# Ten of eleven gate/up chunks as seven products, and down groups that accumulate on a residual copied into PSUM

## The chip, the core and the metric

The kernel runs on one core of a Trainium2 chip. The metric is the time of one execution on the device in microseconds (us); lower is better. The kernel before takes 2157.46 us, the median of three runs (2156.99 to 2157.65). The core has engines that each work through their own queue in order: TensorE (PE; PEld is its loading of weights), VectorE (DVE), ScalarE (ACT), GpSimd (POOL) and SyncE (SP, which here only issues DMAs). Matmuls accumulate in PSUM, which this kernel uses as eight banks of 128 partitions by 512 fp32 numbers.

## What is computed

One layer on x of 256 rows by 2048 columns, all in fp32:

```python
x = layer_norm(ALPHA * x + 0.5 * swiglu(x, ffn1_w1, ffn1_w3, ffn1_w2), ln1_g, ln1_b)
x = layer_norm(ALPHA * x + mixer(x, w_in, ..., w_out), ln2_g, ln2_b)
x = layer_norm(ALPHA * x + 0.5 * swiglu(x, ffn2_w1, ffn2_w3, ffn2_w2), ln3_g, ln3_b)
x = x + sigmoid(x @ w_ple_gate) * (p @ w_ple_proj)
# swiglu(x, w1, w3, w2) = (silu(x @ w1) * (x @ w3)) @ w2
```

w1 and w3 are 2048 x 5632 and w2 is 5632 x 2048. The mixer (a chunked mLSTM beside a stick-breaking attention, between large projections) lies between the two FFNs. The change is almost wholly inside the FFNs.

## The kernel before

**Numbers as pairs.** Each fp32 operand of a matmul is split in two parts, hi and lo, of the type fp32r. For a weight tile of 256 rows by 512 columns (held as 128 x 1024, 512 KB, loaded by one DMA), ACT writes hi (a cast, L1297) and DVE writes lo = raw - hi (L1301): together one *split*. For each 128-row half of the tile there are three matmuls, hi by hi, hi by lo and lo by hi (L1358 to L1360). The six matmuls of one tile against one block of activations are called a *unit* here. Activations are split the same way (L351 and L352, or L359 and L360 behind the four transposes of L357).

**Plain chunks.** The 5632 hidden columns are eleven chunks of 512. Computed plainly, the gate and up projections of a chunk are 16 weight tiles, and each is used by two units, one for each half of the 256 rows: 32 units, 16 splits.

**Sevens.** Gate and up of a chunk can instead be taken as one 2 by 2 block product in the Strassen-Winograd form: seven block products instead of eight, 28 units. Its weight operands are sums of tiles, each used by one unit only, so there are 28 splits, and the sums are made by DVE (L423, 128 x 1024 in SBUF) or by an accumulating DMA that GpSimd issues (L429). The activation side has sums too, made once for each 512 columns of x by four half-width DVE operations (L368, L369, L371, L372), called a *form turn* here. The products come out of PSUM through DVE additions (helper `both`, L633), and products 1 and 2 accumulate in one bank. Before, chunks 0 and 3 are plain and the other nine are sevens.

**Down.** The down projection of a chunk is 16 units with 8 splits, for the output in four column groups and two row blocks. Chunks go in pairs. When a group's bank is done, DVE adds half of it to the residual in SBUF (L685).

**Order.** Python code writes the instructions in the order in which each engine takes them. `main` is a list of units (up of chunk 0, gate of chunk 3, down of chunk 0, and so on); `side` is the nine sevens one behind the other. Behind gate of chunk 0 (16 units) the first 20 units of `main` (HEAD) go alone: the 16 of up of chunk 0 and four of gate of chunk 3. The rest is woven with `side` in proportion. A split is issued as soon as a place among the held splits is free (in an FFN up to 11 raw and 6 split tiles ahead, by the table HELD). Work with a delay (the `sched.spawn` calls, with times from the table DELAY) is put in when the sum of the units' nominal times has passed its due time. At the start of an FFN the activations themselves come in four column parts: in FFN1 they are loaded, in FFN2 they come from the layer norm, whose affine step on the residual is two DVE operations for each part and row block (L596, L598).

**The start.** PE runs 5 + 2 matmuls of ones (WARM, WARM2) before its first unit.

## Time and profile before

| | before |
|---|---|
| median of three runs | 2157.46 us (2156.99 to 2157.65) |
| the profiled execution, span from its first to its last instruction | 2156.9 us |
| the profiled execution's own time | its span; the median is 0.6 us above it |
| PE busy | 2147.3 us, 100% |
| DVE busy | 1897.9 us, 88% |
| ACT busy | 1342.0 us, 62% |
| POOL busy | 157.8 us, 7% |
| DMA | 538 MB, mean 249 GB/s |
| TensorE clock granted | 1.000 on average |

A row of the timeline is: start in us from the span's begin, duration, engine, line, operation, output<-inputs, sizes, number of equal instructions in the row, and in brackets the idle time before it with what ended it. A row of the costliest groups is: line, engine, operation, sizes and count, then busy us in all and the mean in ns of one, then idle time just before them and what ended most of it. A row of the windows is: the stretch, its length, and the busy us (with the count of instructions) of PE, PEld, DVE, ACT and POOL, the granted clock, the mean busy share of the 16 DMA engines and GB/s. Busy times of neighbours overlap a little (an instruction's end is counted to its last write), so the cost of one more instruction is read from the distance of starts in a row of equal ones.

### The profile page before, as it was taken

What the parts mean: (1) busy time and instruction counts of PE and PEld (TensorE: products, weight loads), DVE (VectorE), ACT (ScalarE), POOL (GpSimd) and SP (SyncE); (2) the same over time, 40 slices, a digit from 0 to 9 for tenths busy, and PEclk for the clock granted to TensorE, in tenths of its full rate; (3) what the DMA queues carried; (4) which work ended last, traced back from release to release, by engine and by line L of the source; (5) the groups of instructions that cost most, each with busy time, mean ns of one, the idle gap of its engine ahead of it and who ended that gap; (6) DMA issues with size and microseconds to landing.
All of it is one profiled execution on the core that took longest, in us unless ns stands there. A gap on an engine that the chain in (4) does not pass through costs nothing.

```text
span 2156.9 us, 27553 instructions
## 1 busy us (share of the span) xinstructions
PE 2147.3 (100%) x9758; PEld 1780.6 (83%) x9758; DVE 1897.9 (88%) x2093; ACT 1342.0 (62%) x1652; POOL 157.8 (7%) x186
## 2 busy tenths in 40 slices
PE   9999999999999999999999999999999999999999
PEld 7888888888888888888888888888888888888887
DVE  7899999999998898887888975799999999999974
ACT  6666666666665665677866563556656666656572
POOL 0011000011000000000000000001000011000000
PEclk9999999999999999999999999999999999999999
DMA  8899888999993667877888976579989999999652
GB/s 351 268 274 272 258 270 262 286 272 276 269 325 119 228 211 216 243 221 201 269 266 268 280 253 212 200 195 271 278 246 268 280 276 273 269 264 304 228 174 80
DMA packets 152250, 538.06 MB, mean 249 GB/s; under 512 B 17200, under 2 KB 21808, under 8 KB 152112
## 3 DMA queue, kind: packets, MB, share of 16 engines
q1 hardware_dynamic: 126480, 442.97, 58.5%
q0 software_dynamic: 25632, 93.33, 23.0%
q8 instruction: 76, 1.25, 0.2%
q14 instruction: 62, 0.51, 0.1%
HBM read 529.94 MB, written 6.29 MB: 249 GB/s over the span
## 4 chain that ended last, share of the span: by engine, by line
PE 96%; DVE 2%; issue 1%; ACT 0%; DMA 0%; SPq 0%; DVEq 0%; ACTq 0%
PE mm L1358 31%; PE mm L1360 31%; PE mm L1359 31%; PE ms L357 1%; DVE split L1301 1%; PE ms L566 0%; DVE temp L850 0%; DVE raw L423 0%; PE ms L1017 0%; PE ms L939 0%; PE ms L954 0%; PE ms L1047 0%; DMA big<-in_x_t_dram 0%; ACT split L1297 0%; DVE actT L352 0%
## 5 line engine op out<-in xcount | busy, mean ns | idle before, releaser
L1301 DVE TENSOR_TENSOR split<-raw,split 128x1024 fp32r<-128x1024 f32 (+1 forms) x1090 | 1277.7, 1210 | 130.4 <-ACT split L1297 121.3
L1297 ACT CAST split<-raw 128x1024 fp32r<-128x1024 f32 (+1 forms) x1090 | 1090.0, 1043 | 476.8 <-DVE raw L423 153.3
L1358 PE MATMUL mm<-split,actT 128*128 128x512 f32 x3064 | 1201.8, 392 | 2.8 <-ACT actT L351 1.9
L1360 PE MATMUL mm<-split,actT 128*128 128x512 f32 x3064 | 1188.9, 388 | 0.0
L1359 PE MATMUL mm<-split,actT 128*128 128x512 f32 x3064 | 1187.7, 388 | 0.4 <-DVE split L1301 0.3
L1360 PEld LDWEIGHTS mm<-split,actT 128*128 128x128 f32 x3064 | 576.1, 188 | 119.5 <-DVE actT L352 0.9
L1358 PEld LDWEIGHTS mm<-split,actT 128*128 128x128 f32 x3064 | 576.6, 188 | 117.5 <-ACT actT L351 2.2
L1359 PEld LDWEIGHTS mm<-split,actT 128*128 128x128 f32 x3064 | 576.9, 188 | 114.2 <-DVE split L1301 1.2
L423 DVE TENSOR_TENSOR raw<-raw 128x1024 f32<-128x1024 f32 x190 | 231.4, 1219 | 1.6
L429 POOL DMA_DIRECT2D raw<-in_ffn_w_dram x140 | 122.9, 1009 | 1243.1 <-DVE split L1301 1091.1
L359 ACT CAST actT<-ms 128x512 fp32r<-128x512 f32 x52 | 30.4, 586 | 96.0 <-PE ms L357 90.0
L685 DVE SCALAR_TENSOR_TENSOR big<-mm,big 128x512 f32<-128x512 f32 x112 | 76.4, 684 | 2.3 <-PE mm L1360 2.1
L633 DVE TENSOR_TENSOR temp<-mm,temp 128x512 f32<-128x512 f32 x108 | 73.1, 686 | 2.4 <-PE mm L1360 1.2
L429 POOL DMA_DIRECT2D raw<-in_w_in_dram x38 | 33.3, 1000 | 516.0 <-DVE split L1301 323.6
L292 ACT ACTIVATE temp<-mm 128x512 f32<-128x512 f32 (+1 forms) x36 | 20.3, 570 | 58.6 <-PE mm L1360 58.6
L360 DVE TENSOR_TENSOR actT<-ms,actT 128x512 fp32r<-128x512 f32 x52 | 35.6, 688 | 15.6 <-ACT actT L359 15.5
L352 DVE TENSOR_TENSOR actT<-temp,actT 128x512 fp32r<-128x512 f32 (+1 forms) x42 | 27.3, 675 | 17.3 <-ACT actT L351 17.2
L288 ACT ACT_TABLE_LOAD x30 | 38.5, 1283 | 0.5
L1162 DVE SCALAR_TENSOR_TENSOR big<-big,mm 128x512 f32<-128x512 f32 x8 | 5.5, 686 | 30.9 <-PE mm L1360 30.9
L351 ACT CAST actT<-temp 128x512 fp32r<-128x512 f32 (+1 forms) x42 | 24.7, 610 | 9.4 <-DVE temp L369 8.7
L1217 DVE TENSOR_TENSOR temp<-temp,big 128x512 f32<-128x512 f32 (+1 forms) x10 | 5.8, 583 | 26.4 <-ACT temp L292 26.4
L292 ACT ACTIVATE rstd<-mv,eps 128x1 f32<-128x1 f32 x6 | 1.8, 295 | 42.7 <-DVE mv L549 42.7
(127 smaller groups left out, 601.7 us busy)
## 6 DMA issues: line engine op xcount, KB each, us to landing
raw<-in_ffn_w_dram SPq DMA_DIRECT2D x528, 512.0 KB, 6.0
raw<-in_w_in_dram SPq DMA_DIRECT2D x168, 512.0 KB, 5.1
raw<-in_ffn_w_dram POOLq DMA_DIRECT2D x140, 512.0 KB, 9.5
raw<-in_w_in_dram POOLq DMA_DIRECT2D x38, 512.0 KB, 8.5
raw<-in_w_out_dram SPq DMA_DIRECT2D x32, 512.0 KB, 4.6
raw<-in_w_ple_gate_dram SPq DMA_DIRECT2D x32, 512.0 KB, 4.3
raw<-in_w_up_m_dram SPq DMA_DIRECT2D x16, 512.0 KB, 6.2
raw<-in_w_up_sb_dram SPq DMA_DIRECT2D x16, 512.0 KB, 4.5
```

The source lines that it names most:

```text
L288: nc.scalar.preload_act_table_set(table[0])
L359: nc.scalar.copy(dst[:, 0], ps[:])
L360: nc.vector.tensor_tensor(out=dst[:, 1], in0=ps[:], in1=dst[:, 0], op=ALU.subtract)
L423: nc.vector.tensor_tensor(out=out.tile[:, :, :cols], in0=a.tile[:, :, :cols], in1=b.tile[:, :, :cols], op=ALU.add)
L429: nc.gpsimd.dma_start(out=whole(out.tile[:]), in_=whole(src), accum_op=ALU.add)
L633: nc.vector.tensor_tensor(out=out, in0=a, in1=b, op=op)
L685: nc.vector.scalar_tensor_tensor(out=xs, in0=ps, scalar=0.5, in1=xs, op0=ALU.mult, op1=ALU.add)
L1297: nc.scalar.copy(hi[:, ks], r[:, ks])
L1301: nc.vector.tensor_tensor(out=lo[:, ks], in0=r[:, ks], in1=hi[:, ks], op=ALU.subtract)
L1358: nc.tensor.matmul(ps, hi, w[0][:, k, :u.cols], start=first, stop=False, skip_group_check=u.onto)
L1359: nc.tensor.matmul(ps, hi, w[1][:, k, :u.cols], start=False, stop=False, skip_group_check=u.onto)
L1360: nc.tensor.matmul(ps, lo, w[0][:, k, :u.cols], start=False, stop=last, skip_group_check=u.onto)
```

## The change

In both FFNs only chunk 0 stays plain, and chunk 3 becomes a seven as well. The order of the units is written anew: gate of chunk 0 (16 units), two units of its up projection, the other 14 woven with the first 24 units of the sevens, 8 units of sevens alone, down of chunk 0 woven with the next 34, then each down pair woven with 56 units of sevens. Product 4 accumulates in the bank of product 7, after DVE has added a sum to that bank in place (`both(held[7], held[7], r["u"], ALU.add)`); product 2 now comes before product 4. The down groups start from a bank into which ACT has copied the residual (`seed`, up to five units ahead, while fewer than seven banks are in use), and ACT copies the result back (`put`), so that DVE's L685 is gone; the residual is kept twice as large for this and the last pair's copy halves it. In each seven, but for chunk 1, one sum of tiles that an accumulating DMA made is made by DVE. The mixer's projections that use `seven` get the same treatment of product 4. WARM2 is 11 instead of 2.

```diff
-HEAD = 20
+HEAD = 2
+LAG = 10
+TURNED = 32
+SEED_AHEAD = 5
-WARM2 = 2
+WARM2 = 11
...
@@ load_rows: the residual as it is read
-        activate(res[t, k][:], res[t, k][:], ACT.Copy, scale=ALPHA)
+        activate(res[t, k][:], res[t, k][:], ACT.Copy, scale=2.0 * ALPHA)
@@ four transposes into one bank, only the first with start
+    def turn_four(ps, src):
+        for k in range(4):
+            nc.tensor.matmul(ps[:, k], src[:, k * P:(k + 1) * P], ident[:], is_transpose=True,
+                             start=k == 0, stop=k == 3, skip_group_check=True)
@@ group
+            for u in pairs[-1]:
+                u.onto = seed is not None
+                u.seed = seed if i == 0 else None
@@ seven
-        accs[2] = accs[1]
+        accs[2], accs[4] = accs[1], accs[7]
...
-            m2 = Weight(b21, [], [b21])
-            m4 = Weight(b11, [b21], [b11], plus(b11, b11, b21), m6)
+            m2 = Weight(b21, [b21], [])
+            m4 = Weight(b11, [], [b11, b21], plus(b11, b11, b21), m6)
+            m4.needs = [b21]
...
-            then += [unit(4, i, m4, act, 1, 2), unit(2, i, m2, act, 0, 2)]
-            then[-1].onto = True
+            then += [unit(2, i, m2, act, 0, 2), unit(4, i, m4, act, 1, 2)]
@@ up7: what is done with the products
                 elif m == 2:
                     r["g0"] = temp()
                     activate(r["g0"][:], ps, ACT.Silu)
-                    sched.spawn(late(r["u"], r["v"], r["z"], r["g0"]), DELAY["late" if c < n - 1 else "last"])
...
                 elif m == 4:
+                    activate(r["u"][:], ps, ACT.Silu)
+                    sched.spawn(late(r["u"], r["v"], r["z"], r["g0"]), DELAY["late" if c < n - 1 else "last"])
+                elif m == 3:
                     sched.until(lambda: "rest" in r)
-                    both(r["u"][:], ps, r["u"][:], ALU.add)
-                    sched.spawn(silu(r["u"]), DELAY["silu"])
-                elif m == 3:
                     both(r["v"][:], ps, r["v"][:], ALU.subtract)
 
             def rest():
-                both(r["u"][:], held[7], r["u"][:], ALU.add)
-                both(r["z"][:], held[5], r["u"][:], ALU.add)
+                both(r["z"][:], held[7], r["v"][:], ALU.add)
+                both(held[7], held[7], r["u"][:], ALU.add)
                 r["rest"] = True
...
-            return seven(..., (range(c == 1, 4), range(c == 1, 4)))
+            return seven(..., (range(c == 1, 4), range(1, 4)))
@@ down
-                def add(ps, t, g=g):
-                    xs = xres(t, g * COL)
-                    nc.vector.scalar_tensor_tensor(out=xs, in0=ps, scalar=0.5, in1=xs,
-                                                   op0=ALU.mult, op1=ALU.add)
+                def put(ps, t, g=g):
                     if n - 1 in chunks:
+                        activate(xres(t, g * COL), ps, ACT.Copy, scale=0.5)
                         norm.chunk(t, g)
+                    else:
+                        nc.scalar.copy(xres(t, g * COL), ps)
+
+                def seed(ps, t, g=g):
+                    nc.scalar.copy(ps, xres(t, g * COL))
@@ the order of an FFN
-        gate, hidden = zip(*(up(c) for c in (0, 3)))
-        program.extend((skewed(gate[0][:SKEW]) if skew else flat(gate[0][:SKEW])) + flat(gate[0][SKEW:]))
-        main = flat(hidden[0] + gate[1] + down(0) + hidden[1] + down(1, 2) + down(3, 4) + down(5, 6) + down(7, 8))
-        side = in_line([up7(c) for c in (1, 2, 4, 5, 6, 7, 8, 9, 10)])
-        program.extend(main[:HEAD] + weave(main[HEAD:], side))
+        gate, hidden = up(0)
+        program.extend((skewed(gate[:SKEW]) if skew else flat(gate[:SKEW])) + flat(gate[SKEW:]))
+        side = in_line([up7(c) for c in range(1, n)])
+        program.extend(flat(hidden)[:HEAD])
+        program.extend(weave(flat(hidden)[HEAD:], side[:24]) + side[24:TURNED])
+        main, side = flat(down(0)), side[TURNED:]
+        for c in range(1, n - 2, 2):
+            at = 56 + (LAG - TURNED) * (c == 1)
+            program.extend(weave(main, side[:at]))
+            main, side = flat(down(c, c + 1)), side[at:]
+        program.extend(weave(main, side))
@@ the driver's loop over units
+    def open_bank(u):
+        u.acc["ps"] = ps_pool.tile([P, COL], F32, name="mm", tag="ps")
+        live.add(id(u.acc))
+        if u.seed:
+            u.seed(u.acc["ps"][:, :u.cols], u.tt)
+
+    def seeds_due(n):
+        for u in units[n:n + SEED_AHEAD]:
+            if u.seed and "ps" not in u.acc and len(live) < PSUM_BUFS - 1:
+                open_bank(u)
...
-            first, last = u.start and k == 0, u.stop and k == 1
+            first, last = u.start and k == 0 and not u.seed, u.stop and k == 1
```

Over the whole program the instructions change as follows: PE has 48 matmuls of 128x512 fewer (9000 to 8952) and nine matmuls of ones more; DVE has 24 splits more (1070 to 1094), 34 sums of tiles more (190 to 224) and about 125 operations of 512 columns fewer (L685's 112 to 5 among them); ACT has 24 casts more, 112 copies from SBUF into PSUM more, and about 119 copies or activations from PSUM more; GpSimd issues 2 accumulating DMAs fewer.

Two places show how the order on DVE moves. The first is the start of FFN1, right behind the first form turn (the four rows with `temp<-big` or `temp<-temp,big` are such a turn); `split<-raw,split` are weights' lo parts, `raw<-raw` sums of weight tiles, `actT<-temp,actT` lo parts of forms. Before:

```order
L1301 TENSOR_TENSOR split<-raw,split 128x1024 x5
L352 TENSOR_TENSOR actT<-temp,actT 128x512 x2
L1301 TENSOR_TENSOR split<-raw,split 128x1024 x2
L368 TENSOR_TENSOR temp<-big 128x256
L369 SCALAR_TENSOR_TENSOR temp<-temp,big 128x256
L371 TENSOR_TENSOR temp<-big 128x256
L372 TENSOR_TENSOR temp<-big,temp 128x256
L1301 TENSOR_TENSOR split<-raw,split 128x1024 x2
L352 TENSOR_TENSOR actT<-temp,actT 128x512 x2
L1301 TENSOR_TENSOR split<-raw,split 128x1024 x2
```

After (L1317 is the former L1301, L438 the former L423, L358 the former L352, L378 to L382 the form turn):

```order
L1317 TENSOR_TENSOR split<-raw,split 128x1024 x2
L438 TENSOR_TENSOR raw<-raw 128x1024
L1317 TENSOR_TENSOR split<-raw,split 128x1024 x2
L438 TENSOR_TENSOR raw<-raw 128x1024 x2
L1317 TENSOR_TENSOR split<-raw,split 128x1024
L358 TENSOR_TENSOR actT<-temp,actT 128x512 x2
L1317 TENSOR_TENSOR split<-raw,split 128x1024 x2
L378 TENSOR_TENSOR temp<-big 128x256
L379 SCALAR_TENSOR_TENSOR temp<-temp,big 128x256
L381 TENSOR_TENSOR temp<-big 128x256
L382 TENSOR_TENSOR temp<-big,temp 128x256
L1317 TENSOR_TENSOR split<-raw,split 128x1024 x4
```

Between the first form turn and the second, DVE had seven splits and has seven splits and three sums of tiles now.

The second place is the start of FFN2, where the affine steps of the layer norm (`big<-big`) go on among the first weights. Before, up to the operation ahead of the first form turn there:

```order
L596 SCALAR_TENSOR_TENSOR big<-big 128x512
L598 SCALAR_TENSOR_TENSOR big<-big 128x512
L1301 TENSOR_TENSOR split<-raw,split 128x1024 x2
L596 SCALAR_TENSOR_TENSOR big<-big 128x512
L598 SCALAR_TENSOR_TENSOR big<-big 128x512
L1301 TENSOR_TENSOR split<-raw,split 128x1024 x2
L596 SCALAR_TENSOR_TENSOR big<-big 128x512
L598 SCALAR_TENSOR_TENSOR big<-big 128x512
```

After:

```order
L609 SCALAR_TENSOR_TENSOR big<-big 128x512
L611 SCALAR_TENSOR_TENSOR big<-big 128x512
L1317 TENSOR_TENSOR split<-raw,split 128x1024
L438 TENSOR_TENSOR raw<-raw 128x1024
L1317 TENSOR_TENSOR split<-raw,split 128x1024
L609 SCALAR_TENSOR_TENSOR big<-big 128x512
L611 SCALAR_TENSOR_TENSOR big<-big 128x512
L1317 TENSOR_TENSOR split<-raw,split 128x1024
L438 TENSOR_TENSOR raw<-raw 128x1024 x2
L1317 TENSOR_TENSOR split<-raw,split 128x1024
L609 SCALAR_TENSOR_TENSOR big<-big 128x512
L611 SCALAR_TENSOR_TENSOR big<-big 128x512
```

Three sums of tiles now stand among the affine steps and ahead of the first form turn of FFN2, where there was none; the splits in this piece are four in both.

50 lines of the change are left out of this document (26 added, 24 removed).

## The prediction

> **What bounds the kernel now.** I read the busy times first, then the chain of waits, then the costliest groups of instructions.
>
> ```profile
> PE 2147.3 (100%) x9758; PEld 1780.6 (83%) x9758; DVE 1897.9 (88%) x2093; ACT 1342.0 (62%) x1652; POOL 157.8 (7%) x186
> PE 96%; DVE 2%; issue 1%; ACT 0%; DMA 0%; SPq 0%; DVEq 0%; ACTq 0%
> L1301 DVE TENSOR_TENSOR split<-raw,split 128x1024 fp32r<-128x1024 f32 (+1 forms) x1090 | 1277.7, 1210 | 130.4 <-ACT split L1297 121.3
> L423 DVE TENSOR_TENSOR raw<-raw 128x1024 f32<-128x1024 f32 x190 | 231.4, 1219 | 1.6
> L685 DVE SCALAR_TENSOR_TENSOR big<-mm,big 128x512 f32<-128x512 f32 x112 | 76.4, 684 | 2.3 <-PE mm L1360 2.1
> ```
>
> PE sets the time: it is busy all of the span and 96% of the chain is its own. A busy PE need not be a fast one, so I look at its pitch in mid FFN1.
>
> ```profile
> 419.81 0.39 PE L1358 MATMUL mm<-split,actT 128*128 128x512 f32 x1
> ...
> 427.97 0.39 PE L1358 MATMUL mm<-split,actT 128*128 128x512 f32 x1
> ```
>
> Between these starts lie 36 matmuls: 8.16/36 = 0.2267 us each, so a unit of six takes 1.360 us. A matmul taken away is worth that, as long as DVE, second with 88%, can feed the rest. Windows of 10 us at the start of FFN2 show what that mean hides.
>
> ```profile
> 1390.00:1400.00 10.00, 10.00 (x45) 8.29 (x45) 9.86 (x13) 5.04 (x6) 0.00 (x0) 1.00 0.61 208
> 1400.00:1410.00 10.00, 10.00 (x45) 8.27 (x44) 9.97 (x16) 7.24 (x9) 0.00 (x0) 1.00 0.36 121
> 1410.00:1420.00 10.00, 10.00 (x46) 8.28 (x45) 9.93 (x17) 3.04 (x4) 1.75 (x2) 1.00 0.54 116
> 1420.00:1430.00 10.00, 10.00 (x50) 8.29 (x49) 10.00 (x12) 8.51 (x11) 0.00 (x0) 1.00 0.68 188
> ```
>
> Both are full (PE's 10.00, DVE's 9.86 to 10.00): DVE works 39.8 of 40 us and PE has not yet had to wait. More DVE work per unit of PE becomes time here, once the slack is used.
>
> **What one DVE instruction costs.** Busy times of neighbours overlap, so I take distances between starts.
>
> ```profile
> 32.91 4.63 DVE L1301 TENSOR_TENSOR split<-raw,split 128x1024 fp32r<-128x1024 f32 x4 [0.22 <-DMA raw<-in_ffn_w_dram]
> 37.46 1.29 DVE L352 TENSOR_TENSOR actT<-temp,actT 128x512 fp32r<-128x512 f32 x2
> 38.67 2.36 DVE L1301 TENSOR_TENSOR split<-raw,split 128x1024 fp32r<-128x1024 f32 x2
> ...
> 1397.97 0.69 DVE L596 SCALAR_TENSOR_TENSOR big<-big 128x512 f32<-128x512 f32 x1
> 1398.69 0.69 DVE L598 SCALAR_TENSOR_TENSOR big<-big 128x512 f32<-128x512 f32 x1
> 1399.30 0.42 DVE L368 TENSOR_TENSOR temp<-big 128x256 f32<-128x256 f32 x1
> ...
> 1400.77 2.35 DVE L1301 TENSOR_TENSOR split<-raw,split 128x1024 fp32r<-128x1024 f32 x2
> ```
>
> Four splits take 37.46 - 32.91 = 4.55, 1.137 each. A sum of tiles (L423) has the same size and mean (1219 against 1210 ns), so 1.137 too. A 512-column operation takes (38.67 - 37.46)/2 = 0.605 (0.607 over many pairs, which I use). An affine pair is 1399.30 - 1397.97 = 1.33, a form turn 1400.77 - 1399.30 = 1.47.
>
> **How far DVE is ahead of PE at these places.** The lead is the start of the matmul that needs a split less the end of that split; the smallest in a unit counts.
>
> ```profile
> 31.47 1.23 DVE L1301 TENSOR_TENSOR split<-raw,split 128x1024 fp32r<-128x1024 f32 x1 [5.43 <-ACT split L1297]
> 34.01 0.39 PE L1359 MATMUL mm<-split,actT 128*128 128x512 f32 x1
> ...
> 1381.04 0.69 DVE L352 TENSOR_TENSOR actT<-big,actT 128x512 fp32r<-128x512 f32 x1 [1.85 <-ACT actT L351]
> 1383.72 0.39 PE L1360 MATMUL mm<-split,actT 128*128 128x512 f32 x1
> ...
> 1426.54 2.35 DVE L1301 TENSOR_TENSOR split<-raw,split 128x1024 fp32r<-128x1024 f32 x2
> 1429.30 0.39 PE L1359 MATMUL mm<-split,actT 128*128 128x512 f32 x1
> ```
>
> In FFN1, at its 19th unit (the third of chunk 0's up projection, where the new order starts to differ), the lead is 34.01 - 32.70 = 1.3. In FFN2, ten units after its first, it is 1383.72 - 1381.73 = 2.0. It can't be larger in FFN1, since DVE stood idle for 5.43 just before, waiting for ACT. The third pair tests the tally: from 1381.73 to the end of the first split of the last DVE row (1427.76) the order has 19 splits and 3 sums (25.0), 12 operations of 512 columns (7.3), six affine pairs (8.0) and four form turns (5.9), 46.2 in all; the trace has 46.03.
>
> **PE's part.** 48 matmuls fewer: 48 x 0.2267 = -10.9. All 48 lie in the FFNs (four units each).
>
> **The start.** PE runs nine matmuls of ones more before its first unit.
>
> ```profile
> 1.13 3.35 PE L1235 MATMUL ms<-ones 128*128 128x128 f32 x14 [1.13 <-DVE ones L296]
> 6.35 0.80 PE L1358 MATMUL mm<-split,actT 128*128 128x512 f32 x1 [1.87 <-ACT actT L351]
> ...
> 12.07 0.53 PE L1359 MATMUL mm<-split,actT 128*128 128x512 f32 x1
> 12.43 0.40 PE L1360 MATMUL mm<-split,actT 128*128 128x512 f32 x1
> 12.67 0.40 PE L1358 MATMUL mm<-split,actT 128*128 128x512 f32 x1
> ```
>
> The seven of before are 14 records in 3.35, so nine are 18 records: 4.3 at that pace, against an idle gap of 1.87. From 6.35 to 12.43 there are 14.2 pitches of 0.427, then 0.23: a slow clock, ended by work. The bounds: 2.4 lost, if the added matmuls only push the first unit back (4.3 - 1.87), to 2.9 won, if all fourteen slow matmuls come at 0.227. I take -1.0. It reaches past the next term, since ACT's silu behind gate 0 waits for PE and DVE waits for ACT:
>
> ```profile
> 29.91 0.60 ACT L292 ACTIVATE temp<-mm 128x512 f32<-128x512 f32 x1 [6.36 <-PE mm L1360]
> ```
>
> **The start of FFN1.** Behind gate 0's 16 units there were 20 plain ones alone; now the sevens are woven in behind two. A seven's unit needs its own split, and sums beside it; a plain unit shares its split with another. I count DVE's instructions in the order from the one needed at the 19th unit to the one needed at the 91st (before the first product 4 of chunk 2, where the excess is largest): 62 splits and 17 sums (79 x 1.137 = 89.8), 25 operations of 512 columns (15.2) and three form turns (4.4): 109.4. PE's part is 72 units (97.9) and four groups of transposes.
>
> ```profile
> 405.28 0.60 PE L357 MATMUL ms<-ident,temp 128*128 128x128 f32 x4
> 405.63 0.47 PE L1358 MATMUL mm<-split,actT 128*128 128x512 f32 x1
> 405.95 0.39 PE L1359 MATMUL mm<-split,actT 128*128 128x512 f32 x1
> ```
>
> One group puts the second matmul behind it at 405.95 instead of 405.28 + 0.23, so 0.44; PE has 97.9 + 1.8 = 99.7. DVE needs 9.7 more than PE and has a lead of 1.3: PE waits **8.4**. Before, the same 72 units needed 52 splits, 11 sums, 22 operations and three turns, 89.4, which PE's 98.8 covered.
>
> **The start of FFN2.** The same order, with the layer norm's affine steps on top. From the 11th unit to the 91st DVE has 66 splits and 17 sums (94.4), 26 operations of 512 columns (15.8), six affine pairs (8.0) and four form turns (5.9): 124.1. PE has 80 units and the transposes, 108.8 + 1.8 = 110.6. The excess is 13.5, the lead 2.0: PE waits **11.5**. Most comes in one wait: the 23rd unit is the first that needs a form, and up to it DVE has 25.4 where PE has twelve units, 16.3, so the wait there is 25.4 - 16.3 - 2.0 = 7.1. Before, no form was needed in the first 36 units.
>
> **What moves and costs nothing.** Over the program DVE gains 24 splits and 34 sums (58 x 1.137 = 66) and loses about 125 operations of 512 columns, 107 of them L685 (76): lighter by 10, so behind the two starts it stays near its present share. The in-place sum in PSUM (`mm<-mm,temp`) is not in the trace: between 0.607 and a split's 1.137; I take 0.607 (same columns); there are two in each stretch, 1 more at most. ACT's 112 seeds are not in the trace either (a copy into PSUM): between 0 more and the 1.05 of a cast twice as wide.
>
> ```profile
> L1297 ACT CAST split<-raw 128x1024 fp32r<-128x1024 f32 (+1 forms) x1090 | 1090.0, 1043 | 476.8 <-DVE raw L423 153.3
> L639 ACT COPY temp<-mm 128x512 f32<-128x512 f32 x18 | 10.6, 586 | 15.7 <-PE mm L1360 15.6
> ```
>
> By the 586 ns of a copy from PSUM, 112 seeds and 119 put-backs are 135 and 24 casts 25: ACT goes from 1342 to about 1500, 70%. Behind a seed on ACT wait casts, and so splits; with 30% idle I cost it at nothing. Without that cover each seed and put-back would put the casts behind it off by 1.2, 130 over both FFNs.
>
> DMA: the FFN1 stretch issues two more loads on SP's queue and three more accumulating ones on POOL's than the same units before.
>
> ```profile
> 25.00:135.00 110.00, 110.00 (x491) 91.08 (x490) 98.11 (x106) 69.37 (x80) 10.59 (x12) 1.00 0.90 287
> ```
>
> Five transfers of 524 KB at 287 GB/s are 9 us beside 0.90 of 98.8; the stretch is longer by 8.4, so the share is about 0.91. It hides.
>
> **The sum.** 2157.46 - 10.9 - 1.0 + 8.4 + 11.5 = 2165.5. The profiled execution's span, 2156.9, lies 0.6 below the median; I carry that along.
>
> **The rivals.**
>
> *PE's count decides (faster or the same).* DVE's excess at the two starts would be absorbed, for instance by splits made further ahead while PE still works through gate 0 and the mixer's tail. For it: DVE is 88% busy over all, and 10 more of lead at each place would do. Against it: the window rows at FFN2's start, full already, and the 5.43 idle that DVE spends on ACT. Whole: 2157.46 - 11.9 = 2145.6; half absorbed: 2155.6.
>
> *PE waits for the bank of product 7 (slower still).* Product 4 may start only after DVE's in-place sum, which stands behind product 6's two sums and a difference: four operations (2.4) and a split or two (1.1 to 2.3), against about four units in between, product 3's last and product 2's first with those woven among them (5.4). Where it doesn't fit, 0.5 to 1 us in each of 20 sevens of the FFNs and five of the mixer: 12 to 25 on top, 2178 to 2190. It decides once DVE is more than 2 late there. For it, DVE's share in the FFNs:
>
> ```profile
> 100.00:200.00 100.00, 100.00 (x446) 82.85 (x446) 96.97 (x97) 64.26 (x70) 12.24 (x14) 1.00 0.93 278
> 400.00:500.00 100.00, 100.00 (x450) 82.86 (x450) 94.32 (x94) 61.86 (x66) 8.78 (x10) 1.00 0.91 272
> ```
>
> Against: 3.5 to 4.7 of work fit in 5.4.
>
> *The pause slows the clock.* The 7.1 wait in FFN2 could bring back the 0.427 pitch that followed the idle 1.87 at the start; by those rows, up to 14 matmuls at 0.2 more, 2.9: 2168.4. The Trainium skill ("TensorE: Matmul & The Clock Gate", section "What's actually happening") says that an idle window of about 3.4 us halves the clock and as long a busy one restores it; the rows at the start agree with a slow clock after idling, and no row of before shows a pause of that length later on.
>
> That the change doesn't do what it says is out: the order shows the 48 matmuls gone.
>
> **How the numbers follow.** Forecast 0.55 (2165.5; own range 2161 to 2171, from the start's -2.9 to +2.4, the in-place sum's 1 in each stretch and a lead 1 to 2 off), PE's count 0.24 (a third of it whole, two thirds part), the bank 0.13, the clock 0.08. The range reaches to half of the first rival and to the lower half of the bank's: 2149 to 2175. A measurement of this kernel can tell 0.2%, 4.3 us: faster is below 2153.1, slower above 2161.8. Faster: half of PE's count, 0.14. Same: the rest of it and the forecast's lower edge, 0.16. Slower: 0.70.
>
> **What would show it.** PE's matmuls 48 fewer at the same 0.227 pitch. PE idle, released by DVE splits or forms, between 35 and 135 and in the first 110 of FFN2, 8 and 11 in sum, one wait of some 7 at the first form of FFN2, and hardly any elsewhere; DVE at 9.9 of 10 there. No wait of PE on ACT's seeds. Wrong if PE is full in these windows (then DVE was ahead by more, or its work lies elsewhere in time), or if it waits at each product 4.

## The result

The changed kernel takes 2181.8 us (median of four runs, 2178.35 to 2184.69), the kernel before 2157.2 in the same runs: 1.0114 times as long, 95% interval 1.0102 to 1.0126. The forecast was 2165.5, slower, in a range of 2149 to 2175. The direction was right, the size was not: +24.6 instead of +8.

The runs of the change scatter over 6 us, those of before over 1. The profiled execution of the change is its fastest, 2178.35 (span 2176.3); the time outside the span is 2.0 us in it, as in other runs, and the profiled execution of before was itself some 1.7 us slower in its span than the runs that were timed.

The busy times and the chain of waits of the change:

```profile
PE 2148.7 (99%) x9728; PEld 1775.6 (82%) x9728; DVE 1891.6 (87%) x2026; ACT 1473.2 (68%) x1903; POOL 155.8 (7%) x184
PE 83%; DVE 7%; DMA 5%; issue 4%; ACT 1%; POOL 0%; SPq 0%; DVEq 0%; POOLq 0%; ACTq 0%
```

PE's share of the chain fell from 96% to 83%. What it waits for (engine and line, what ended the wait, then us in total, number, longest), of the change and then of before:

```profile
PE mm L1390 <- ACT actT L357: 8.2, 3, 4.8
PE ms L362 <- DVE actT L370: 6.4, 5, 2.2
PE mm L1392 <- DVE actT L358: 3.1, 3, 1.7
PE mm L1390 <- ACT mm L698: 1.8, 1, 1.8
```

```profile
PE mm L1358 <- ACT actT L351: 1.9, 1, 1.9
PE ms L1235 <- DVE ones L296: 1.1, 1, 1.1
PE mm L1358 <- DVE actT L1053: 0.9, 1, 0.9
```

Before, PE waited 4 us in all. Now it waits for forms (L357, L358), for banks that transposes need (L362 behind L370) and once for a seed (L698).

To see where time goes, I take for a stretch the distance between the starts of its first and last unit, less the work in it (0.2267 for each matmul of 512 columns, 0.11 for each transpose); what is left is called its loss here. For the change's two critical stretches:

```profile
32.30 0.39 PE L1390 MATMUL mm<-split,actT 128*128 128x512 f32 x1
...
146.15 0.39 PE L1390 MATMUL mm<-split,actT 128*128 128x512 f32 x1
...
1393.63 0.39 PE L1390 MATMUL mm<-split,actT 128*128 128x512 f32 x1
...
1517.53 0.50 PE L1390 MATMUL mm<-split,actT 128*128 128x512 f32 x1
```

146.15 - 32.30 - 99.7 = 14.2 in FFN1 (units 19 to 91) and 1517.53 - 1393.63 - 110.6 = 13.3 in FFN2 (units 11 to 91). The same for all stretches and profiles that the text speaks of:

| profile | FFN1 19-91 | FFN1 91-151 | rest of FFN1 | FFN2 11-91 | FFN2 91-157 | rest of FFN2 |
|---|---|---|---|---|---|---|
| before | 0.1 | 0.1 | 0.4 | 0.0 | 0.1 | 1.1 |
| the change | 14.2 | 2.4 | 1.4 | 13.3 | 1.9 | 0.6 |
| the change, second profile (e1) | 13.9 | 5.0 | 0.5 | 14.0 | 2.3 | 4.9 |
| e2: nine sevens | 0.1 | 0.1 | 1.8 | 0.0 | 0.2 | 1.9 |
| e7: nine, product 4 as before | 0.1 | 0.1 | 0.4 | 0.0 | 0.1 | 0.8 |
| e5: without eight sums an FFN | 12.8 | 4.7 | 1.5 | 12.0 | 1.9 | 2.4 |
| e9: without early accumulating loads | 10.4 | 0.3 | 0.9 | 13.1 | 0.3 | 1.0 |
| e17: their traffic without the wait | 10.4 | 0.3 | 1.7 | 13.0 | 1.7 | 1.1 |
| e10: without either | 4.8 | 0.1 | 1.5 | 9.1 | 0.1 | 1.1 |
| e3: affine steps later | 13.8 | 4.5 | 1.7 | 18.5 | 3.9 | 0.6 |
| e11: forms earlier | 11.8 | 4.0 | 0.4 | 17.6 | 2.3 | 0.9 |
| e12: both | 11.9 | 2.7 | 1.3 | 18.6 | 2.1 | 4.1 |
| e15: put back by DVE | 13.9 | 1.8 | 1.7 | 18.1 | 1.8 | 2.8 |

The mixer between the FFNs differs by less than 0.4 among these profiles. The account of the profiled execution closes: start -1.5, matmuls -10.9, the six columns' differences to before +14.1, +2.3, +1.0, +13.3, +1.8 and -0.5, together 19.6, against 2176.3 - 2156.9 = 19.4.

**FFN2's wait for the first form.** DVE, ACT and PE of the change:

```profile
1408.51 2.35 DVE L438 TENSOR_TENSOR raw<-raw 128x1024 f32<-128x1024 f32 x2
...
1414.77 2.35 DVE L1317 TENSOR_TENSOR split<-raw,split 128x1024 fp32r<-128x1024 f32 x2
1417.04 1.29 DVE L358 TENSOR_TENSOR actT<-temp,actT 128x512 fp32r<-128x512 f32 x2
```

```profile
1409.72 0.39 PE L1392 MATMUL mm<-split,actT 128*128 128x512 f32 x1
1414.89 0.79 PE L1390 MATMUL mm<-split,actT 128*128 128x512 f32 x1 [4.78 <-ACT actT L357]
1415.48 0.63 PE L1391 MATMUL mm<-split,actT 128*128 128x512 f32 x1
1417.78 0.79 PE L1392 MATMUL mm<-split,actT 128*128 128x512 f32 x1 [1.67 <-DVE actT L358]
```

PE loses 1414.89 - 1409.72 - 0.23 = 4.9 and 1417.78 - 1415.48 - 0.23 = 2.1: 7.0, where the forecast had 7.1, at the unit that it named. DVE runs without a gap there (from 1395 to 1495 it is busy for 99.45 of 100). Behind the wait the matmuls come at 0.43 for some 5 us, and the windows show the clock:

```profile
60.00:80.00 20.00, 16.89 (x65) 13.18 (x64) 18.23 (x22) 11.36 (x14) 0.90 (x2) 0.87 0.85 246
1400.00:1420.00 20.00, 13.55 (x52) 10.37 (x51) 19.83 (x25) 12.09 (x14) 1.75 (x2) 0.82 0.60 157
```

**FFN1 is another matter.** In the first of these two windows DVE is not full: 18.2 of 20. ACT and PE around the second form there:

```profile
68.51 1.05 ACT L1313 CAST split<-raw 128x1024 fp32r<-128x1024 f32 x1 [4.61 <-DMA raw<-in_ffn_w_dram]
71.54 1.99 ACT L1313 CAST split<-raw 128x1024 fp32r<-128x1024 f32 x2 [1.98 <-DMA raw<-in_ffn_w_dram]
73.44 1.14 ACT L357 CAST actT<-temp 128x512 fp32r<-128x512 f32 x2
```

The form turn was done on DVE at 68.5, but its cast on ACT (L357) stands in the queue behind the casts of weights, and these wait 4.61 and 1.98 for a loaded tile. DVE's half of the splits waits for the same casts. The chain of waits has a load of 11.8 us there, from 59.71 to 71.47: an accumulating one, issued by GpSimd at 59.16.

### The profile page after: what moved, and what is told of

Read it like the earlier page. It is cut to its first block, busy times and chain, and to the rows that moved or that the text cites. A ratio compares the mean times of both kernels' runs of the same rounds, so it can differ in the third digit from the quotient of the medians.

```text
span 2176.3 us, 27666 instructions
## 1 busy us (share of the span) xinstructions
PE 2148.7 (99%) x9728; PEld 1775.6 (82%) x9728; DVE 1891.6 (87%) x2026; ACT 1473.2 (68%) x1903; POOL 155.8 (7%) x184
## 4 chain that ended last, share of the span: by engine, by line
PE 83%; DVE 7%; DMA 5%; issue 4%; ACT 1%; POOL 0%; SPq 0%; DVEq 0%; POOLq 0%; ACTq 0%
PE mm L1390 27%; PE mm L1392 27%; PE mm L1391 26%; DMA raw<-in_ffn_w_dram 5%; DVE split L1317 4%; PE ms L362 1%; DVE raw L438 1%; ACT split L1313 1%; DVE actT L358 0%; DVE temp L866 0%; DMA big<-in_x_t_dram 0%; POOL raw L444 0%; DVE temp L646 0%; PE ms L1033 0%; PE ms L955 0%
## 5 line engine op out<-in xcount | busy, mean ns | idle before, releaser
L1317 DVE TENSOR_TENSOR split<-raw,split 128x1024 fp32r<-128x1024 f32 (+2 forms) x1114 | 1306.9, 1210 | 147.1 <-ACT split L1313 138.9
L1313 ACT CAST split<-raw 128x1024 fp32r<-128x1024 f32 (+2 forms) x1114 | 1119.6, 1043 | 393.8 <-DVE raw L438 127.4
L1390 PE MATMUL mm<-split,actT 128*128 128x512 f32 (+1 forms) x3048 | 1197.4, 393 | 11.4 <-ACT actT L357 8.2
L1392 PE MATMUL mm<-split,actT 128*128 128x512 f32 (+1 forms) x3048 | 1184.2, 389 | 3.2 <-DVE actT L358 3.1
L1391 PE MATMUL mm<-split,actT 128*128 128x512 f32 (+1 forms) x3048 | 1182.6, 388 | 0.2
L438 DVE TENSOR_TENSOR raw<-raw 128x1024 f32<-128x1024 f32 x224 | 273.1, 1220 | 3.0
L695 ACT COPY big<-mm 128x512 f32<-128x512 f32 x96 | 56.3, 588 | 58.6 <-PE mm L1392 58.0
L298 ACT ACTIVATE temp<-mm 128x512 f32<-128x512 f32 (+1 forms) x54 | 31.1, 581 | 62.6 <-PE mm L1392 62.6
L698 ACT COPY mm<-big 128x512 f32<-128x512 f32 x112 | 66.1, 593 | 0.0
L369 ACT CAST actT<-ms 128x512 fp32r<-128x512 f32 x52 | 30.4, 587 | 42.8 <-PE ms L362 42.8
L646 DVE TENSOR_TENSOR temp<-mm,temp 128x512 f32<-128x512 f32 x80 | 54.8, 685 | 0.7
L370 DVE TENSOR_TENSOR actT<-ms,actT 128x512 fp32r<-128x512 f32 x52 | 35.5, 686 | 14.9 <-ACT actT L369 14.9
L358 DVE TENSOR_TENSOR actT<-temp,actT 128x512 fp32r<-128x512 f32 (+1 forms) x42 | 27.3, 675 | 20.9 <-ACT actT L357 20.9
L362 PE MATMUL ms<-ident,temp 128*128 128x128 f32 x176 | 26.7, 274 | 6.4 <-DVE actT L370 6.4
L362 PEld LDWEIGHTS ms<-ident,temp 128*128 128x128 f32 x176 | 21.3, 139 | 13.8 <-DVE actT L370 9.0
```

The lines of the kernel that those rows point to most:

```text
L362: nc.tensor.matmul(ps[:, k], src[:, k * P:(k + 1) * P], ident[:], is_transpose=True, start=k == 0, stop=k == 3, skip_group_check=True)
L370: nc.vector.tensor_tensor(out=dst[:, 1], in0=ps[:], in1=dst[:, 0], op=ALU.subtract)
L438: nc.vector.tensor_tensor(out=out.tile[:, :, :cols], in0=a.tile[:, :, :cols], in1=b.tile[:, :, :cols], op=ALU.add)
L646: nc.vector.tensor_tensor(out=out, in0=a, in1=b, op=op)
L695: nc.scalar.copy(xres(t, g * COL), ps)
L698: nc.scalar.copy(ps, xres(t, g * COL))
```

## The experiments

All are variants of the changed kernel, but for e8. Their kernels before ran on the same chip beside them, at 2156.9 to 2157.3.

**e1, the change once more.**

> The changed kernel itself, unchanged, for a second profile beside the runs of this group. Theory A (DVE's excess at the two starts gives pauses, and some pauses bring the slow TensorE clock back): the same pauses at the first forms and in down of chunk 0, about 22 us of PE waiting in sum, and a number of slow-clock stretches that may differ from the three of the first profile, 2.2 us each; 2178 to 2185. Theory B (the pauses are chance, a disturbed run): pauses at other places.

2182.1 (2181.3 to 2185.0), 1.0114 (1.0098 to 1.0131). The same pauses at the first forms (8.3 and 3.1 us, for 8.2 and 3.1 in the first profile) and much the same at transposes (7.7 for 6.4), and a stretch of slow matmuls more (four, some 7 us in sum, where the first profile had three, 6.5). New are two waits for the in-place sum at product 4, 2.9 in sum, where the first profile had 0.2. The loss is not a disturbed run.

**e2, nine sevens again.** The order of before, the rest as changed:

```diff
-HEAD = 2
+HEAD = 20
-        gate, hidden = up(0)
+        gate, hidden = zip(*(up(c) for c in (0, 3)))
...
+        side = in_line([up7(c) for c in (1, 2, 4, 5, 6, 7, 8, 9, 10)])
+        program.extend(main[:HEAD] + weave(main[HEAD:], side))
```

> Only the order and the count of sevens undone: chunks 0 and 3 plain, HEAD 20, the rest as changed (seeds, put-back by ACT, product 4 on the bank of 7, WARM2 11). Theory A (ten sevens and their order cause all of the loss, since DVE is then never behind PE at the starts): no PE pauses over 1 us, no slow clock, 2157.2 - 1.7 (the start, as the profile of the change has it) = 2155.5, and DVE busy about 1830. Rival (seeds and the bank of product 7 cost time by themselves, since transposes waited for a bank): PE waits at transposes remain, 5 to 7 us, 2161 to 2163.

2159.8 (ten runs, 2159.3 to 2161.3), 1.0013 (1.0003 to 1.0022). Two pauses of 0.8 are new against before, and there is no slow clock. So the tenth seven with its order makes 2182 - 2159.8 = 22 of the 24.6, and since it also takes 10.9 of matmuls away, it costs 33 elsewhere. The rest is 2.5 where I expected -1.7. Transposes do not wait here, so the rival's reason is wrong too; what waits is product 4:

```profile
PE mm L1384 <- DVE mm L646: 1.3, 2, 0.7
```

**e7, nine sevens with product 4 as before; e8, the kernel before with the longer start alone.** e7 puts back `seven`, `both7` and `up7` of before, so product 4 has its own bank and DVE adds it, products 2 and 4 change places again, and 16 sums of tiles go back from DVE (206 to 190) to accumulating loads (124 to 140); e8 is `WARM2 = 11` on the kernel before.

> Nine sevens in the order of before, with seeds, put-back by ACT and WARM2 11, but product 4 in its own bank and added by DVE as before. If the 2.5 that the nine-seven variant is above the kernel before are waits for the in-place sum at product 4 (two of 1.05 in its profile): 2156 to 2157.5, with no wait at a product's first unit. If seeds or copies cost it: 2159.5 again.

> The kernel before with WARM2 11 alone. By the start of the nine-seven variant (first unit 0.5 later, all its matmuls at 0.23, PE 1.13 ahead from the 9th unit on): -1.1, 2156.1. Rival (the gain is given back where PE waits for DVE or ACT next): 2157.2.

e7: 2156.3 (ten runs, 2155.8 to 2157.0), 0.9996 (0.9987 to 1.0006). e8: 2157.06, 0.9999 (0.9990 to 1.0009). What e7 puts back is thus what the nine-seven variant lost, 3.4 by the medians. The two waits for the in-place sum, 0.8 each beyond the pitch, are seen in e2's profile and gone from e7's; the rest is smaller pieces (the table's 1.8 and 1.9 against 0.4 and 0.8), and how it divides between the bank and the 16 sums was not tested. e7 is the fastest kernel of this study, but its 0.8 cannot be told from no change. The longer start alone did not bring the 1.1 that I expected from it; 0.1 is within the scatter. In e8's own profile PE keeps a lead of 1.1 to 1.2 on the profile of before, from the 19th unit of FFN1 to the 91st of FFN2, so the rival's later wait is not seen there; but that profile of before is itself slower than the timed runs, by 1.7, and the gain stays unsettled.

**e3, e11, e12: other due times.** The affine steps of FFN2 put off, the form turns 10 us earlier, and both:

```diff
-    norm2 = Norm(ln2_g[0], ln2_b[0], gb2, x2T, 2.0 * ALPHA, (4.0, 1.0))
+    norm2 = Norm(ln2_g[0], ln2_b[0], gb2, x2T, 2.0 * ALPHA, (26.0, 3.0))
...
-    ... "form": 18.0, ...
+    ... "form": 8.0, ...
```

> The change with the layer norm's affine steps ahead of FFN2 put off (their due times 26 + 3 per step instead of 4 + 1), so that they no longer stand before the first form turn. Theory A, the tally of DVE's work: the wait at the first form of FFN2 falls from 7.0 to about 0.5, but the same work comes later and the excess by the 68th unit of FFN2 is as large as before or 2 larger, so PE waits as long in smaller pieces; only the slow clock of 2.2 may go: 2179 to 2184. Rival (the wait is one late form, local): 7 + 2.2 less, 2172 to 2173.

> The change with the form turns due 10 us earlier (8 instead of 18), so that DVE makes them while gate 0 runs, where it is idle for part of the time. If DVE's idle time there takes them: the two or three pauses at first forms (7.0 in FFN2, 5.6 in FFN1, with their slow stretches) shrink by 6 to 10: 2170 to 2176. If the work only moves ahead of splits that PE needs as soon: 2179 to 2185, with pauses at gate 0's or up 0's units.

> Form turns 10 us earlier and the affine steps of FFN2 later, both. By the tally the affine steps' 8 us come back in the 40 units behind, as they did alone; so 0 to 4 beside the run with early forms alone.

2185.8, 2182.5 and 2186.1 (1.0131, 1.0120, 1.0134, each to about 0.0015). None of these three orders of the same work is faster; e11 loses 2 less in FFN1's first stretch and 4 more in FFN2's. In e3 the wait at FFN2's first form fell from 7.0 to 2.5 (the tally had 0.5), and the stretch's loss rose from 13.3 to 18.5: eight smaller waits took its place, the longest of 4.6 for the in-place sum at product 4. So the wait is a sum of DVE's work, not one late form. That the loss rose by 4.5 to 5.2 and not by 2 at most is beyond the tally.

**e5, less work for DVE.** The sums of product 6 of the first two sevens left out:

```diff
+            if rows == D and ca in (COL, 2 * COL):
+                m6 = Weight(b11, [b22] if i in loaded[1] else [], [])
```

> The change without the DVE sums for product 6 in the first two sevens of each FFN (eight sums an FFN left out, so product 6 of these two chunks uses the operand of product 5 and the output is not the reference's). Theory A (DVE's excess at the starts makes the pauses): the tally's excess falls to 3.5 in FFN1 and 7.3 in FFN2, less the leads 2.2 and 5.3 of waiting instead of 8.4 and 11.5; with fewer waits at transposes and fewer slow-clock stretches 2158 to 2170. Rival (banks, or loads that come late, make the waits): within 3 of the change's 2182.

2179.8 (2179.6 to 2181.5), 1.0107: only 2.3 less, where 12 and more were expected. Here my theory that DVE's work explains all waits fell. DVE's waits from 30 to 200 us, in e5 and then in the change:

```profile
DVE split L1319 <- ACT split L1315: 18.0, 20, 3.6
```

```profile
DVE split L1317 <- ACT split L1313: 8.5, 10, 3.6
```

DVE did not get ahead with the 9 us that it saved; it waited 9.5 more for ACT's casts, and ACT waited for loads (19.9 us from 30 to 200, 22.1 in the change).

**e9 and e10: without accumulating loads.** GpSimd's accumulating DMAs of the first three sevens of each FFN left out (e9), 40 in all, so that these sums lack a term; and e5's edit on top (e10):

```diff
+                if not (rows == D and ca in (COL, 2 * COL, 3 * COL)):
                     nc.gpsimd.dma_start(out=whole(out.tile[:]), in_=whole(src), accum_op=ALU.add)
```

> The change without the accumulating DMAs of the first three sevens of each FFN (about 22 an FFN left out, so these sums lack a term and the output is not the reference's). Theory B (the first sevens follow each other too closely for their accumulating loads of 9 to 12 us, ACT's cast waits for them, and the forms' and transposes' casts stand behind it): the pauses at 71, 125, 183 of FFN1 and 1497, 1554 of FFN2 go, 8 to 10 us with a slow stretch or two, 2168 to 2174; the wait of 7 at the first form of FFN2 stays. Theory A (DVE's work alone): unchanged, 2179 to 2185.

> The same with the sums for product 6 of the first two sevens left out as well (output not the reference's). If both causes stand one behind the other (take one away and the other waits): only the first form of FFN2 still waits, 5 to 7 us and 2 of slow clock; the nine-seven variant's 2159.75 less 48 matmuls is 2148.9, so 2154 to 2160. If neither is the cause: 2177 or more.

e9: 2170.7 (2169.7 to 2172.0), 1.0064 (1.0049 to 1.0079), 11.4 less than the change. ACT's waits for loads from 30 to 200, 22.1 us, are gone. e10: 2161.6 (2159.5 to 2163.8), 1.0022 (1.0012 to 1.0031), 20.5 less. So the same sums that were worth 2.3 alone are worth 9.1 once no load is waited for: two limits stand one behind the other, and taking one away uncovers the other. FFN1's units 91 to 151 lose 0.3 instead of 2.4 to 5. What stays in e10 is FFN2's first form:

```profile
PE mm L1393 <- ACT actT L357: 5.9, 2, 4.8
PE mm L1395 <- DVE actT L358: 2.3, 2, 1.7
```

That wait is 7.0 here as well, though one sum fewer stands ahead of it: DVE waits for ACT's cast instead, and the cast waits for the sum that DVE has just made, a round trip with nothing between.

```profile
1397.11 1.22 DVE L438 TENSOR_TENSOR raw<-raw 128x1024 f32<-128x1024 f32 x1
...
1398.37 2.94 ACT L1316 CAST split<-raw 128x1024 fp32r<-128x1024 f32 x3 [1.28 <-DVE raw L438]
...
1399.44 1.22 DVE L1320 TENSOR_TENSOR split<-raw,split 128x1024 fp32r<-128x1024 f32 x1 [1.11 <-ACT split L1316]
```

**e13, e16, e17: awaited, or in the way?** The loads of e9 could have acted by their traffic. In e13 they go into spare tiles that nothing reads (two tile pages fewer for it), in e16 a copy goes to DRAM, in e17 a copy from the lo tile of the split just made goes to DRAM:

```diff
+                if rows == D and ca in (COL, 2 * COL, 3 * COL):
+                    to = spare[len(turns) % 4]
+                    turns.append(0)
+                    nc.gpsimd.dma_start(out=to[:], in_=whole(latest[0][:]))
```

> As the run without accumulating loads in the first three sevens, but these DMAs are issued all the same, into two spare buffers that nothing reads (two tile pages fewer for them; the sums lack a term, the output is not the reference's). If waiting for the accumulated tile itself made the pauses: 2169 to 2173 like the run without them. If the traffic delays the ordinary loads behind which ACT waits: 2179 to 2185 like the change; between the two in parts.

> As the run without accumulating loads in the first three sevens, but a plain copy of the same 512 KB, from the same place and issued at the same moment by GpSimd, goes to a spare buffer in DRAM, so the traffic stays (with a write to DRAM instead of one to SBUF) and nothing waits for it (the sums lack a term, the output is not the reference's). If the accumulated tiles' lateness made the pauses: 2169 to 2173. If the traffic delays the ordinary loads behind which ACT waits: 2178 to 2185. The run before it on this question had two tile pages fewer and was slow in gate 0 and the mixer already, which this one does not touch.

> As the run without accumulating loads in the first three sevens, but in the place of each a copy of the same 512 KB goes from the lo tile of the split just made to a spare buffer in DRAM. It waits for that split, as the accumulating load does, so the traffic comes at the same time; nothing waits for it, only the page of the tile is held some us longer (the sums lack a term, the output is not the reference's). In the two runs before on this question GpSimd issued its DMAs at the program's start, since nothing held them back, and they made the loads of gate 0 late. If the pauses come from waiting for the accumulated tile: 2169 to 2174, with FFN1's units 90 to 150 free of waits. If from the traffic: 2178 to 2185, with the waits in units 90 to 150 back.

e13 and e16 took 2210.5 and 2210.4: with nothing but the spare tiles to wait for, GpSimd issued twenty of its DMAs from 1.9 to 37 us (e16), and gate 0's loads came late beside them. PE's first 50 us of e16 (the window's columns as above):

```profile
0.00:50.00 50.00, 23.63 (x84) 17.72 (x85) 10.51 (x16) 11.82 (x17) 10.93 (x27) 0.72 0.96 343
```

They tell nothing on the question but how tight the loads are at the program's start. e17 held them to their time: 2172.7 (2172.2 to 2173.2), 1.0073 (1.0056 to 1.0090), 2.0 above e9 and 9.4 below the change, with the same 10.4 and 0.3 in FFN1 as e9. So the accumulating loads cost mostly by being awaited. The 2.0 is the price of e17's traffic, which is not quite theirs: it runs from SBUF to DRAM and adds nothing up, and the DMA share from 30 to 200 is 0.83 with it, 0.92 in the change and 0.64 in e9.

How such a wait reaches PE shows at 183 us of the change (ACT, DVE and PE):

```profile
181.24 1.06 ACT L1313 CAST split<-raw 128x1024 fp32r<-128x1024 f32 x1 [2.62 <-DMA raw<-in_ffn_w_dram]
...
183.67 0.57 ACT L369 CAST actT<-ms 128x512 fp32r<-128x512 f32 x1
...
184.94 0.68 DVE L370 TENSOR_TENSOR actT<-ms,actT 128x512 fp32r<-128x512 f32 x1
...
185.68 0.66 PE L362 MATMUL ms<-ident,temp 128*128 128x128 f32 x4 [2.18 <-DVE actT L370]
```

ACT's cast waits for the load; the cast of the last transposes (L369) and DVE's lo part of them (L370) stand behind it, among further splits and a seed; until then their bank is held, and PE's next transposes, which need it, wait. PE's queue is in order, so the matmuls behind wait too.

**e6, later seeds.** Seeds only while fewer than five banks are in use (`len(live) < PSUM_BUFS - 3`):

> The change with seeds allowed only while fewer than five banks are in use, not seven. If the five waits at transposes (7.7 in the second profile) come from banks that early seeds hold: these waits fall to about 2, 2175 to 2178. If they come from DVE's lateness in freeing the bank of the transposes before (theory A): no change within 2, or some more where a seed now comes too late for its first unit, 2181 to 2186.

2269.9, 1.0522 (1.0504 to 1.0539): 88 slower. No transposes wait any more, but PE waits for seeds at 34 places:

```profile
PE mm L1390 <- ACT mm L698: 79.9, 34, 5.9
PE mm L1390 <- ACT actT L357: 7.7, 3, 4.8
```

So seeds have to be early. That the transposes waited for banks which early seeds hold is not shown by e6 alone, since PE is so late there that the other engines get ahead. But e15, which has no seeds, has no wait at transposes either, and e10, which has the seeds and less for DVE and ACT to wait for, has 0.5 of it. My reading that either lateness or banks must be at work was too simple: these runs fit the two together.

**e15, the put-back on DVE again.** No seeds, the residual at its old scale, `scalar_tensor_tensor` as before:

> The change with the down groups put back by DVE as before (no seeds, residual at its old scale). By the tally DVE's excess grows from 9.7 to 13.5 by the 118th unit of FFN1 and from 13.5 to 17.2 in FFN2, about 4 more of waiting in each, and DVE gets 65 us more work in all, which takes mid FFN from 95% to about 99%: 2189 to 2200. Rival (seeds and copies by ACT make waits of their own that are worth more): 2175 to 2182.

2184.2 (2182.7 to 2185.4), 1.0125: 2 slower than the change, not 7 or more. FFN2's first stretch lost 18.1 instead of 13.3 to 14.0, the 4 of the tally; FFN1's did not change: DVE's waits for casts there fell from 3.5 to 1.2, so part of the added work went into time in which DVE had waited. DVE's 60 us more (1951 busy) in mid FFN did not show.

**e4 and e14, the slow clock.** Dummy matmuls of ones fill the waits at the first forms, in part (e4, with 16 in place of 21 and without the second piece) and whole (e14, shown):

```diff
+        for _ in range({22: 6, 986: 21}.get(done_units, 0)):
+            nc.tensor.matmul(ps[:, :P], ones[:], ones[:], start=True, stop=True)
...
+            if k == 0 and done_units in (22, 986):
+                warm({22: 2, 986: 8}[done_units])
```

> The change with dummy matmuls of ones (6 ahead of the first unit on forms in FFN1, 16 in FFN2, into the bank that this unit then starts anew), so that PE is busy while it waits there. If idling brings the slow clock: no stretch of 0.427 pitch behind these two places, -1.8 and -2.2, so about 4 less than the change: 2178. If the slow clock has another cause: the same stretches, no difference, or up to 3 more where the dummies outlast the wait.

> The change with the two waits at the first forms filled wholly: 6 dummies ahead and 2 inside in FFN1, 21 ahead and 8 inside in FFN2. If idling brings the slow clock: no 0.427 stretch behind either place and about 4 less than the change, 2178. If it comes from something else: the stretches stay, 2182 or somewhat more.

In e4 the stretch of 0.427 matmuls behind the first form of FFN1 was gone, the one in FFN2 was there again behind the 1.2 and 2.2 of idling that were left. In e14 both were gone. The change's windows at the two places, and then those of e14:

```profile
30.00:50.00 20.00, 18.26 (x72) 14.22 (x71) 19.70 (x22) 13.26 (x16) 3.65 (x4) 0.91 1.03 346
1400.00:1420.00 20.00, 13.55 (x52) 10.37 (x51) 19.83 (x25) 12.09 (x14) 1.75 (x2) 0.82 0.60 157
```

```profile
30.00:50.00 20.00, 19.82 (x95) 16.19 (x94) 19.62 (x22) 13.36 (x17) 3.65 (x4) 1.00 1.04 345
1400.00:1420.00 20.00, 19.55 (x115) 16.93 (x114) 19.83 (x25) 12.36 (x14) 1.75 (x2) 1.00 0.57 155
```

The granted clock is 1.00 instead of 0.91 and 0.82: in FFN2 PE's idling brings the slow clock. In FFN1 this is weaker, since e3, e5 and e17 have the pause there unfilled and no slow stretch behind it. But the time did not fall: 2183.4 (2177.0 to 2187.9) and 2184.1 (2181.4 to 2186.2), 1.0120 and 1.0125. Behind FFN2's first form e14 has waits of 2.6 and 1.6 for the in-place sum at product 4, ended at 1460 and 1518, where the change's first profile has 0.2 and none. That fits a stretch which DVE and the loads pace, where a slower PE only waits less; with the scatter of these runs it is not shown, only that four microseconds of clock did not come back.

## Why the prediction was wrong in size

By its own terms:

- **PE's part, -10.9:** the matmuls are gone at the same pitch. Right.
- **The start, -1.0:** PE is 1.5 ahead at the 19th unit of the change and 1.1 in e2. Behind 32 records of ones the matmuls come at 0.23 almost at once. Right between the profiles; alone (e8) it isn't seen in the time.

```profile
1.13 6.39 PE L1251 MATMUL ms<-ones 128*128 128x128 f32 x32 [1.13 <-DVE ones L302]
7.27 0.47 PE L1390 MATMUL mm<-split,actT 128*128 128x512 f32 x1
7.58 0.39 PE L1391 MATMUL mm<-split,actT 128*128 128x512 f32 x1
```

- **The start of FFN2, 11.5:** measured 13.3 and 14.0, in them 2.2 and 1.5 of slow clock; the single wait of 7.1 came as 7.0. Right, and e3 showed it to be a sum of work.
- **The start of FFN1, 8.4:** measured 14.2 and 13.9, and 2.4 to 5.0 behind it where the forecast had nothing. This is the step that failed. The tally let DVE work there without a gap ("DVE at 9.9 of 10"), and the sentence on DMA, "It hides", put the loads at nothing. I weighed the five more loads as a share of bandwidth (0.91) and did not ask what waits for each accumulating one: ACT's cast, behind it in ACT's queue the casts of forms and of transposes, and DVE's half of the splits. From 35 to 135, before, in the change and in e9:

```profile
35.00:135.00 100.00, 100.00 (x447) 82.79 (x446) 93.76 (x101) 64.27 (x74) 10.59 (x12) 1.00 0.89 275
35.00:135.00 100.00, 92.11 (x388) 73.87 (x387) 96.24 (x103) 68.98 (x82) 11.46 (x13) 0.95 0.93 266
35.00:135.00 100.00, 93.46 (x405) 74.87 (x405) 99.62 (x106) 71.47 (x85) 0.00 (x0) 0.98 0.61 206
```

  ACT waited for loads before too, 13.4 us from 30 to 150 against 15.4 now, and DVE was idle for 6.2 of these 100 us, but PE was full: DVE had time to spare. Now it has none, since of the stretch's 72 units 49 belong to sevens instead of 32, and what it waits comes on top of its work: 3.5 of waits for casts and the tally's 8.4 are 11.9 of the 14.2. Without the awaited loads DVE is at 9.96 of 10 and waits 0.2, and the stretch loses 10.4. With the tally's 2.2 for eight sums fewer, the same addition gives 5.3 for e10 (2.2 + 3.1; measured 4.8) and 13.7 for e5 (2.2 + 11.5; measured 12.8); over these four profiles it is off by 0.5 to 2.3. If the slow clock in e9 and e17, 1.8 and 1.2, counts whole, which e14 does not show, 8.6 and 9.2 are left of their 10.4, next to the tally's 8.4; so close a match is partly luck. By e9 and e17 the awaited loads are 3.5 to 3.8 of FFN1's first stretch, 2 to 5 of its next and 0.5 to 3 in FFN2. In the time they are 11.4 (e9) or 9.4 (e17) of the 16.3 that the forecast missed; the 2170.7 of e9 lies in the forecast's own range of 2161 to 2171.
- **The in-place sum, at most 1 in each stretch:** its duration was right, 0.60 by the starts 432.05, 432.65 and 433.25 of e2's DVE. What it makes PE wait was the rival on the bank of product 7, to which I gave 12 to 25 and a chance of 0.13. It exists: two waits of 0.8 in e2, at most 3.4 over the whole program with the 16 sums (e2 against e7). Where DVE is late it grows, as the rival said: 0.2 and 2.9 us of idling in the two profiles of the change, 5.7 in e15, 5.8 in e14 and 8.3 in e3.

```profile
432.05 0.68 DVE L646 TENSOR_TENSOR temp<-mm,temp 128x512 f32<-128x512 f32 x1
432.65 0.69 DVE L646 TENSOR_TENSOR mm<-mm,temp 128x512 f32<-128x512 f32 x1
433.25 0.68 DVE L646 TENSOR_TENSOR temp<-mm,temp 128x512 f32<-128x512 f32 x1
```

- **The seeds, at nothing:** a seed takes 593 ns, and one wait of 1.8 for a seed is in the profile. They cost nothing only because they are issued up to five units early: e6 shows 80 us of waits without that. And they hold banks: the five waits at transposes, 6.4 us, were no part of the forecast. I weighed ACT's idle time and not the banks.
- **The slow clock** was a rival at 0.08 and at one place. It came in both profiles of the change, in three and four stretches of 6.5 and some 7 us in sum; the shortest pauses ahead of one are 1.14 and 0.61 of idling within 3 us. What it adds to the time is not shown (e14).

```profile
39.08 0.50 PE L1390 MATMUL mm<-split,actT 128*128 128x512 f32 x1 [1.14 <-ACT actT L357]
39.42 0.40 PE L1391 MATMUL mm<-split,actT 128*128 128x512 f32 x1
40.43 0.63 PE L1392 MATMUL mm<-split,actT 128*128 128x512 f32 x1 [0.61 <-DVE actT L358]
40.85 0.63 PE L1390 MATMUL mm<-split,actT 128*128 128x512 f32 x1
```

- **PE's count decides** is out: nothing absorbed DVE's excess. Where DVE had less to do (e5), the wait for ACT's casts took its place.
- **Range and chances:** the range was said to reach into the lower half of the bank's rival, 2178 to 2190, but ended at 2175, below it; and half of 0.24 is 0.12, not 0.14.

The remaining 3.5 between the profiled execution and the median lie in waits that come and go: the second profile has 2.6 more in units 91 to 151 and 4.3 more in the rest of FFN2. Which load or bank is late by chance there was not tested.

The Trainium skill ("TensorE: Matmul & The Clock Gate", section "What's actually happening") has the clock fall after an idle window of about 3.4 us and calls the window free-running. The second would fit: pauses of the same length (1.1 to 1.2 and 0.6) at 38 us were followed by slow matmuls in both profiles of the change and not in e3's. The first is not borne out as a bound on one pause, since 1.75 us of idling in two pieces was enough.

## What to carry to other kernels

Count the work of the engine that is second behind the bound stage by stage, with its lead as the slack: that told the place and size of FFN2's wait to 0.1 us. But a count of work is only a lower bound where a chain of queues feeds the engine: waits that cost nothing while the engine has time to spare are added to its work once it has none. So look up in the trace of before how long that engine stands idle and for what, and ask of each load, of accumulating ones above all, what else stands behind the instruction that waits for it. And when one suspected limit is taken away without gain, take the next one away together with it before the first is acquitted: here eight sums an FFN were worth 2.3 alone and 9.1 behind the loads.

## What the runs showed of the hardware

- Granted clock: pauses of PE of 1 to 5 us were followed, not always, by 2 to 5.5 us of matmuls at 0.427 instead of 0.227 (in the change from 76.2 to 81.7, in e17 from 1412.9 to 1415.0, in e3 none behind 1.18 and 0.61 at 39 us); with dummies in the pause the clock stayed at 1.00 (e14).
- An accumulating DMA of 512 KB, issued by GpSimd, took 11.8 us on the chain of waits (59.71 to 71.47) and 8.9 in the median from issue to landing, a plain one of SyncE 5.5 (both of the change's profile).
- DMAs of GpSimd that wait for no compute run at once and delay SyncE's loads: forty of 512 KB, twenty of them in the first 50 us, cost some 40 us (e16 against e9), and the three loads of `in_x_t` of 512 KB took 29.1 us in the median instead of 7.8.
- A copy of 128x512 from SBUF into PSUM on ACT takes 593 ns, from PSUM 588; an in-place DVE sum in PSUM costs the same 0.60 as one into SBUF (e2, by the starts 432.05 to 433.25).
